# The inverse of the delta rule, on 128x128 matmuls or on blocks of 32 and 64 rows

## The chip, the cores and the metric

The kernel runs on one core of a Trainium2 chip. The metric is device time in microseconds of one execution. A core has TensorE (matmuls into PSUM; the profile shows its weight loads as PEld), VectorE (DVE), ScalarE (ACT), GpSimd (POOL) and SyncE (SP, which here only issues DMAs).

## The reference

A trunk of two layers on 256 tokens of width 2048, in float32. Layer 0 mixes the tokens by eight heads of a gated delta rule beside a pooling mixer, layer 1 by a convolution module; each is followed by a squared-ReLU MLP. The change touches the delta rule alone, of which this is the part that matters:

```python
def gated_delta_rule(q, k, v, g, beta):
    ...
    gamma = jnp.exp(jnp.where(causal, gc[..., :, None] - gc[..., None, :], -jnp.inf))
    kb = k * beta[..., None]
    a_mat = jnp.where(strict, jnp.einsum('bhnck,bhnmk->bhncm', kb, k) * gamma, 0.0)
    t_inv = lax.linalg.triangular_solve(a_mat + eye, jnp.broadcast_to(eye, a_mat.shape),
                                        left_side=True, lower=True, unit_diagonal=True)
    u = jnp.einsum('bhncm,bhnmv->bhncv', t_inv, v * beta[..., None])
    w = jnp.einsum('bhncm,bhnmk->bhnck', t_inv, kb * jnp.exp(gc)[..., None])
```

So each piece of tokens needs the inverse of a unit lower triangular matrix. The reference cuts the sequence into pieces of 64 tokens; the kernel uses pieces of 128, two per head.

## The kernel before

Weights stream from HBM as tiles `w` of 128x2048 (`load`, 1 MB each). ScalarE makes a rounded high part `wh`, VectorE the rest `wl`, in halves of 1024 columns. A `gemm` adds 48 passes of 256 columns into a PSUM bank `mm`: high by high, high by low, low by high, over 16 blocks of the contraction.

Layer 0's mixer is in `even`. The eight heads go in four rounds of two. A round has `keys` (projections and normalized keys), `front` (values, queries, gates), `inverse` and `finish` (the recurrence over the two pieces, and the head's output). The rounds overlap: the projections of the next round are computed while the inverse of this one runs. The order of all instructions on each engine is fixed when the program is built, by a scheduler with its own cost estimates; `inverse` and `finish` stand under `tc.high_priority()`. After the last round `pooling` follows; its eight gemms may run earlier, but what it writes as operand for the output projection lies in the same memory as the inverse's scratch tile `scr`, so that part comes after the last `finish`.

`inverse` handles four 128x128 matrices at once (two heads, two pieces), side by side in 512 columns. `a` is minus the strictly lower matrix, `aT` its transpose by TensorE. It keeps the inverse `t` and the transposed inverse `tT`, both full size. It starts with the diagonal blocks of 4 rows: `b` and `bT` are `a` and `aT` with all else masked out, and with their square `xs` the product (1+b)(1+b^2) is the inverse there. Then five levels double the block from 4 to 128 rows. On a level `xs` is `a` times `t` (bank `px`, copied by ScalarE), `pq` is `t` times `xs` and `pr` its transpose; two predicated copies on VectorE with masks from `msks` put the new blocks into `t` and `tT`. On the last level only `tT` is needed, as the weights of the two matmuls in `finish`. All of these matmuls are f32 with 128 rows and 128 columns of weights and 128 moving columns, which the program writes in groups of four (`ch<-scr 128x128`). The banks `ch` are two, used in turn.

Of the kernel before, what the change touches and what calls it, by code (L numbers as in the profile page):

```python
# [7 lines left out]
F32 = mybir.dt.float32  # L8
# [5 lines left out]
P = 128  # L14
SEQ = 256
# [3 lines left out]
EPS = 1e-6  # L19
BIG = 1e30  # L20
WINDOWS = (2, 4, 8, 16)
LEVELS = (4, 8, 16, 32, 64)

# [19 lines left out]


@with_exitstack
def trunk_kernel(ctx: ExitStack, tc: tile.TileContext, x_in, xT, vec, dwt, posts, ab, cst, msk, inv,
                 ew, eba, epw, ewo, ow, owo, mu, md, out):
    nc = tc.nc  # L50

    cp = ctx.enter_context(tc.tile_pool(name="cp", bufs=1))
# [20 lines left out]
        return op_a_tile[:, k, sl]  # L73

    vecs = cp.tile([P, V_COLS], F32, name="vecs")
    csts = cp.tile([P, 6, P], F32, name="csts")
    abs_ = cp.tile([P, 16], F32, name="abs_")
    invs = cp.tile([P, 4, 16], F32, name="invs")
    msks = cp.tile([P, 9, P], mybir.dt.uint8, name="msks")
    ident, triu, ones, pos, neg, blk = (csts[:, i, :] for i in range(6))  # L80
    mhalf = cp.tile([P, 1], F32, name="mhalf")
    nc.gpsimd.memset(mhalf, -0.5)

# [9 lines left out]
    def bank(tag):  # L93
        return pp.tile([P, 2 * SEQ], F32, tag=tag, name=tag, bufs=4 if tag == "mm" else 2)
# [4 lines left out]
    def stt(out_, a, s, b, op0=ALU.mult, op1=ALU.mult):  # L99
        return nc.vector.scalar_tensor_tensor(out_, a, s, b, op0=op0, op1=op1)  # L100

    def pin(ins):
        return tc.keep_in_program_order(ins)

    def mm(ps, lhsT, rhs, start=True, stop=True):
        nc.tensor.matmul(ps, lhsT, rhs, start=start, stop=stop)  # L106
# [206 lines left out]
    def first_operand(ep, src):  # L313
        w = wp.tile([P, D], F32, tag="w", name="w", bufs=2)
        wh = wp.tile([P, D], F32R, tag="wh", name="wh")
        wl = wp.tile([P, D], F32R, tag="wl", name="wl")
        xqs, cols = [], [slice(512 * i, 512 * i + 512) for i in range(4)]
        for i in range(4):
            xq = sc([P, 4, SEQ], "xq", pool=ep, bufs=4)
            nc.sync.dma_start(xq, xT[:, 4 * i:4 * i + 4, :])  # L320
            nc.sync.dma_start(w[:, cols[i]], src[:, cols[i]])
            xqs.append(xq)
        for k in range(KT):
            split(op_a, k, xqs[k // 4][:, k % 4, :], scale=v(V_MIX_PRE + k))
            if k % 4 == 3:
                c = cols[k // 4]
                nc.scalar.copy(wh[:, c], w[:, c])  # L327
                nc.vector.tensor_sub(wl[:, c], w[:, c], wh[:, c].bitcast(F32))
        return xqs, (wh, wl)
# [17 lines left out]
    def gate_weights():  # L347
        w = wp.tile([P, D], F32, tag="w", name="w", bufs=2)
        nc.sync.dma_start(w[:, :KT * 16], eba)
        wv = w[:, :KT * 16].rearrange("p (k m) -> p k m", m=16)  # L350
        wh = wp.tile([P, D], F32R, tag="wh", name="wh")
        wl = wp.tile([P, D], F32R, tag="wl", name="wl")
        nc.vector.memset(wh.bitcast(F32), 0.0)
        nc.gpsimd.memset(wl.bitcast(F32), 0.0)
        whv = wh.rearrange("p (k m) -> p k m", m=P)[:, :, :16]
        nc.scalar.copy(whv, wv)
        nc.vector.tensor_sub(wl.rearrange("p (k m) -> p k m", m=P)[:, :, :16], wv, whv.bitcast(F32))
        return wh, wl
# [94 lines left out]
    def heads(h0, r, ep, scr, obs, em, beta, nbeta, eg, ek, be):  # L453
# [6 lines left out]
        def quad(ap):  # L460
            return ap.rearrange("p (i t) -> p i t", i=4)

        def all4(mask):
            return mask.unsqueeze(1).to_broadcast([P, 4, P])

        kns, knTs = [], []
        a, aT, b, t = (scr[:, i] for i in range(4))
        spare = [scr[:, 6], scr[:, 7]]


        def keys(first=None):
# [35 lines left out]
        def inverse(tT):  # L507
            ps = bank("ch")
            for i in range(4):
                knT = knTs[i // 2][:, i % 2, :]  # L510
                mm(ps[:, i * P:(i + 1) * P], knT, knT)
            for i in range(4):
                h, c = h0 + i // 2, i % 2
                stt(a[:, i, :], ps[:, i * P:(i + 1) * P], nbeta[:, c, h:h + 1], em[:, h, 0, c, :])
            ps = bank("ch")
            for i in range(4):
                nc.tensor.transpose(ps[:, i * P:(i + 1) * P], a[:, i, :], ident)
            nc.scalar.copy(aT, quad(ps))

            bT, xs = spare  # L520
            nc.vector.tensor_mul(b, a, all4(blk))
            nc.vector.tensor_mul(bT, aT, all4(blk))
            nc.vector.tensor_add(t, b, all4(ident))
            nc.vector.tensor_add(tT, bT, all4(ident))
            ps = bank("ch")
            for i in range(4):
                mm(ps[:, i * P:(i + 1) * P], b[:, i, :], bT[:, i, :])
            nc.scalar.copy(xs, quad(ps))
            pq, pr = bank("ch"), bank("ch")
            for i in range(4):  # L530
                mm(pq[:, i * P:(i + 1) * P], xs[:, i, :], t[:, i, :])
            for i in range(4):
                mm(pr[:, i * P:(i + 1) * P], t[:, i, :], xs[:, i, :])
            nc.vector.tensor_add(t, t, quad(pq))
            nc.vector.tensor_add(tT, tT, quad(pr))

            for lv in range(len(LEVELS)):
                last = lv == len(LEVELS) - 1
                px = bank("ch")
                xs = spare[lv % 2]  # L540
                for i in range(4):
                    mm(px[:, i * P:(i + 1) * P], aT[:, i, :], t[:, i, :])
                nc.scalar.copy(xs, quad(px))  # L543
                if not last:
                    pq = bank("ch")
                    for i in range(4):
                        mm(pq[:, i * P:(i + 1) * P], tT[:, i, :], xs[:, i, :])
                    nc.vector.copy_predicated(t, all4(msks[:, lv, :]), quad(pq))
                pr = bank("ch")
                for i in range(4):  # L550
                    mm(pr[:, i * P:(i + 1) * P], xs[:, i, :], tT[:, i, :])
                nc.vector.copy_predicated(tT, all4(msks[:, 4 + lv, :]), quad(pr))


        def finish(tT, tag):
            for hh in range(2):
# [35 lines left out]
                split(obs, h, y)  # L592

        return keys, front, inverse, finish

    def pooling(r, ep, op_b):
# [30 lines left out]
    def even():  # L627
        with tc.tile_pool(name="fp", bufs=2) as fp:
            wh, wl = gate_weights()
            xqs, first = first_operand(fp, ew[HEADS])  # L630
            r = first_norm(fp, xqs)
        with tc.tile_pool(name="ep", bufs=2) as ep:
            scr = cp.tile([P, 8, 4, P], F32, tag="op_b1", name="scr")
            decays, *gs = gates(r, wh, wl, ep)
            for h in range(2):
                decays(h, "ch")
            mraw = scr[:, :3].rearrange("p i c t -> p (i c t)")[:, :9 * P].rearrange("p (i t) -> p i t", t=P)
            pin(nc.gpsimd.dma_start(mraw, msk))
            pin(nc.gpsimd.tensor_copy(msks, mraw))
            lower = cp.tile([P, KT // 2, 2 * SEQ], F32R, tag="op_b0", name="op_b0")  # L640
            rounds = [heads(h, r, ep, scr, lambda k, sl: lower[:, k, sl], *gs) for h in range(0, HEADS, 2)]
            rounds[0][0](first)
            for i, (_, front, inverse, finish) in enumerate(rounds):
                front()
                if i + 1 < len(rounds):
                    for h in range(max(2 * i + 2, 2), 2 * i + 4):
                        decays(h, "sm")
                    rounds[i + 1][0]()
                with tc.high_priority():
                    inverse(scr[:, 4 + i % 2])  # L650
                    finish(scr[:, 4 + i % 2], "ch" if i + 1 == len(rounds) else "sm")
            upper = cp.tile([P, KT // 2, 2 * SEQ], F32R, tag="op_b1", name="op_b1")

            def op_b(k, sl):
                return (lower if k < KT // 2 else upper)[:, k % (KT // 2), sl]

            pooling(r, ep, op_b)
        return op_b
# [125 lines left out]

    nc.gpsimd.dma_start(vecs[:, :V_NEAR], vec[:, :V_NEAR])
    nc.gpsimd.dma_start(csts, cst)
    nc.gpsimd.dma_start(abs_, ab)
    nc.gpsimd.dma_start(invs, inv)
    xd = dp.tile([P, 2, D], F32, name="xd", bufs=1)
# [97 lines left out]
```

## Time and profile before

| | |
|---|---|
| median of three runs | 2254.94 us (2253.87 to 2256.69) |
| the profiled execution | 2253.11 us, its span 2251.3 us |
| granted TensorE clock, mean | 0.987 |
| TensorE busy | 2194.6 us, 97% |
| VectorE, ScalarE busy | 1350.2 us (60%), 1030.2 us (46%) |
| DMA | 414.46 MB, mean 184 GB/s |

All times inside a profile count from the start of the span. A row of a group gives line, engine, operation, tiles written and read, shapes and count. A TensorE row of the form `128*32 128x256` has 128 rows and 32 columns of weights, and a result of 256 columns. One f32 matmul leaves two records, one fp32r matmul one. In a table by stretch the columns are the stretch, its length, then busy time and count for TensorE, weight loads, VectorE, ScalarE and GpSimd, the granted clock, the DMA share and GB/s. A bracket at a timeline row's end is the time that the engine sat idle before it and who released it.

### The profile page before, as it was taken

Reading aid. Unit: us, or ns where it says so; the run is one execution under the profiler, and the core shown is the slowest. Engines: PE = TensorE matmul, PEld = TensorE weight load, DVE = VectorE, ACT = ScalarE, POOL = GpSimd, SP = SyncE. Lnnn points to the kernel's source line nnn. Section 1 sums busy time; section 2 is a strip of 40 time slices with the busy share of each in tenths; the row PEclk is TensorE's granted clock in tenths of the full one; section 3 lists DMA queues with packets and bytes.
Section 4 is the critical chain, followed back from the end, with each engine's and each line's share of the span. In section 5 each row is a group of like instructions: output and inputs, shape, how many; then the busy total and the mean of one; then the engine's idle time right before and its main releaser. Section 6 shows DMA issues by size and latency. Waiting matters only on the chain.

```text
span 2251.3 us, 32079 instructions
## 1 busy us (share of the span) xinstructions
PE 2194.6 (97%) x13228; PEld 1915.9 (85%) x13228; DVE 1350.2 (60%) x1926; ACT 1030.2 (46%) x1569; POOL 125.5 (6%) x200
## 2 busy tenths in 40 slices
PE   8999998999999999999999999799999999999997
PEld 8999997888888888888878999588888888888886
DVE  7767674576456456556556777557645645655654
ACT  6646554454444344334434333445444434443442
POOL 3201000000000000000002222000000000000000
PEclk9999999999999999999999999899999999999999
DMA  6433334645555555555547887454555555555553
GB/s 220 144 130 132 116 129 155 238 169 205 188 188 189 197 193 187 188 190 194 195 150 229 228 228 220 163 208 172 202 196 194 188 187 189 192 197 188 188 189 110
DMA packets 67378, 414.46 MB, mean 184 GB/s; under 512 B 13952, under 2 KB 14112, under 8 KB 20000
## 3 DMA queue, kind: packets, MB, share of 16 engines
q1 hardware_dynamic: 55440, 391.27, 48.9%
q0 software_dynamic: 11792, 21.15, 4.1%
q8 instruction: 103, 1.69, 0.3%
q14 instruction: 43, 0.35, 0.0%
HBM read 405.75 MB, written 6.55 MB: 183 GB/s over the span
## 4 chain that ended last, share of the span: by engine, by line
PE 94%; DVE 2%; issue 1%; ACT 1%; DMA 1%; POOL 0%; POOLq 0%; DVEq 0%; SPq 0%; ACTq 0%
PE mm L106 87%; PE ch L106 3%; PE sm L705 2%; PE sm L106 1%; DVE wl L131 1%; DMA w<-ew 0%; DVE op_a L100 0%; ACT L97 0%; PE sm L441 0%; PE sm L233 0%; PE ch L233 0%; ACT wh L125 0%; DMA xq<-xT 0%; POOL r L190 0%; DVE x L100 0%
## 5 line engine op out<-in xcount | busy, mean ns | idle before, releaser
L131 DVE TENSOR_TENSOR wl<-w,wh 128x1024 fp32r<-128x1024 f32 x720 | 853.7, 1223 | 580.6 <-ACT wh L125 579.7
L106 PE MATMUL mm<-op_a,wh 128*128 128x256 f32 (+1 forms) x4352 | 1148.7, 337 | 0.3 <-ACT wh L327 0.3
L125 ACT CAST wh<-w 128x1024 fp32r<-128x1024 f32 x720 | 720.3, 1049 | 675.7 <-PE mm L106 558.1
L106 PE MATMUL mm<-op_a,wl 128*128 128x256 f32 x3200 | 901.5, 282 | 0.0
L106 PEld LDWEIGHTS mm<-op_a,wh 128*128 128x128 f32 x4352 | 745.1, 189 | 92.8 <-issue 5.5
L106 PE MATMUL mm<-wh,op_b 128*128 128x512 f32 x2560 | 796.0, 392 | 4.9 <-ACT op_b L97 4.5
L106 PEld LDWEIGHTS mm<-op_a,wl 128*128 128x128 f32 x3200 | 604.7, 189 | 3.6 <-issue 2.4
L106 PEld LDWEIGHTS mm<-wh,op_b 128*128 128x128 f32 x2560 | 481.3, 188 | 108.4 <-ACT op_b L97 5.1
L106 PE MATMUL mm<-wl,op_b 128*128 128x512 f32 x1280 | 498.9, 390 | 0.0
L106 PEld LDWEIGHTS mm<-wl,op_b 128*128 128x128 f32 x1280 | 240.9, 188 | 51.4 <-DVE wl L131 0.2
L97 ACT ACTIVATE op_b<-f 128x256 fp32r<-128x256 f32 x128 | 53.3, 418 | 229.6 <-DVE f L100 229.6
L190 POOL TENSOR_TENSOR r<-m,mhalf 128x1 f32<-128x1 f32 x8 | 6.1, 766 | 1615.2 <-DVE m L257 1615.2
L186 DVE TENSOR_TENSOR op_b<-f,op_b 128x256 fp32r<-128x256 f32 x128 | 54.2, 425 | 55.3 <-ACT op_b L97 55.3
L106 PE MATMUL ch<-scr 128*128 128x128 f32 x544 | 68.7, 275 | 0.3 <-ACT scr L543 0.3
L106 PEld LDWEIGHTS ch<-scr 128*128 128x128 f32 x544 | 64.8, 191 | 0.6 <-ACT scr L543 0.5
L705 PE MATMUL sm<-us,wd 128*32 128x256 f32 x752 | 50.5, 394 | 8.8 <-issue 8.8
L300 DVE TENSOR_TENSOR big<-mm,big 128x512 f32<-128x512 f32 x48 | 33.0, 687 | 42.9 <-PE mm L106 42.9
L100 DVE SCALAR_TENSOR_TENSOR f<-h 128x256 f32<-128x256 f32 x128 | 54.2, 425 | 4.0
L289 DVE TENSOR_TENSOR h<-mm,hl 128x256 f32<-128x256 f32 x128 | 53.3, 418 | 0.0
L100 DVE SCALAR_TENSOR_TENSOR near<-u,vecs,near 128x256 f32<-128x256 f32 x104 | 49.2, 480 | 0.9
L705 PEld LDWEIGHTS sm<-us,wd 128*32 128x32 f32 x752 | 25.1, 112 | 26.6 <-issue 12.1
L162 ACT COPY hl<-mm 128x256 f32<-128x256 f32 x128 | 46.1, 362 | 2.7 <-DVE h L289 2.2
(242 smaller groups left out, 893.9 us busy)
## 6 DMA issues: line engine op xcount, KB each, us to landing
w<-mu SPq DMA_DIRECT2D x128, 1024.0 KB, 4.8
w<-md SPq DMA_DIRECT2D x128, 1024.0 KB, 4.8
w<-ew SPq DMA_DIRECT2D x39, 1024.0 KB, 4.8
w<-ow SPq DMA_DIRECT2D x32, 1024.0 KB, 5.4
w<-ewo SPq DMA_DIRECT2D x16, 1024.0 KB, 4.9
w<-owo SPq DMA_DIRECT2D x16, 1024.0 KB, 4.9
us<-ud POOLq DMA_DIRECT2D x64, 140.5 KB, 7.8
wd<-dwt POOLq DMA_DIRECT2D x14, 384.0 KB, 5.9
```

The lines of the kernel that those rows point to most:

```text
L97: return nc.scalar.activation(out_, in_, func, bias=bias, scale=scale, **kw)
L100: return nc.vector.scalar_tensor_tensor(out_, a, s, b, op0=op0, op1=op1)
L106: nc.tensor.matmul(ps, lhsT, rhs, start=start, stop=stop)
L125: ins = nc.scalar.copy(wh[:, c], w[:, c])
L131: ins = nc.vector.tensor_sub(wl[:, c], w[:, c], wh[:, c].bitcast(F32))
L162: nc.scalar.copy(s, ps[:, SEQ:])
L186: return first, nc.vector.tensor_sub(op(k, LO), src, hi)
L190: nc.gpsimd.tensor_tensor(dst, m, mhalf.to_broadcast(m.shape), op=ALU.pow)
L289: nc.vector.tensor_add(h, hh, s)
L300: nc.vector.tensor_add(m, ps[c], m)
L705: nc.tensor.matmul(ps[32 * g:32 * g + 32, :SEQ], wd[:, i, g, :], us[:, g, lo:lo + SEQ], start=i == skip, stop=i == GROUPS - 1, tile_positi ...
```

## The change

The inverse no longer works on whole 128x128 matrices. The four diagonal blocks of 32 rows of each matrix are kept in a compact form: `t32`, 128 partitions by four matrices by 32 columns. They start from blocks of two rows, whose inverse needs no matmul (a constant `sub` picks the one element below the diagonal, `diag` adds the ones). Levels 2, 4, 8 and 16 then work within the blocks, on tiles of 32 rows by 32 columns of the tensor array: `tile_mm` gives the place of the tile, and the four blocks of one matrix lie on the four tiles of the array's diagonal. The transposed factor `tT32` is no longer computed by matmuls of its own, but by a transpose of 32x32 blocks on VectorE after each predicated copy. So a level has 32 matmuls in two groups of 16 instead of 12 of full size, and its copies cover 128 columns instead of 512.

Two steps then join blocks. The 32-row blocks are joined to 64 (one group of 8 and one of 12 tile matmuls), and the 64-row blocks to 128 by two groups of four matmuls on tiles of 64 by 64; in each step only the block off the diagonal is computed, and copied to its place in `tl` or `tT`. The other parts of `tT` and `tl` are never written, so one memset on GpSimd clears them once. The masks shrink from nine of 128 columns to four of 32; the constants lose one matrix and gain the small input `blk`, loaded by a DMA of its own on GpSimd's queue.

```diff
-LEVELS = (4, 8, 16, 32, 64)
+LEVELS = (2, 4, 8, 16)
+ROWS32 = [slice(b, b + 32) for b in range(0, 128, 32)]
...
+        def tile_mm(rows, cols, ps, lhsT, rhs):
+            nc.tensor.matmul(ps[cols], lhsT[rows], rhs[rows], start=True, stop=True,
+                             tile_position=(rows.start, cols.start))
...
-            bT, xs = spare
-            nc.vector.tensor_mul(b, a, all4(blk))
-            nc.vector.tensor_mul(bT, aT, all4(blk))
-            nc.vector.tensor_add(t, b, all4(ident))
-            nc.vector.tensor_add(tT, bT, all4(ident))
-            ps = bank("ch")
+            for b in ROWS32:
+                nc.vector.tensor_mul(t32[b], a[b, :, b], sub[b].unsqueeze(1).to_broadcast([32, 4, 32]))
+            nc.vector.tensor_add(t32, t32, diag.unsqueeze(1).to_broadcast([P, 4, 32]))
+            nc.vector.transpose(flat(tT32), flat(t32))
+            for lv in range(len(LEVELS)):
+                px = bank("ch")
+                for i in range(4):
+                    for b in ROWS32:
+                        tile_mm(b, b, px[:, 32 * i:32 * i + 32], aT[:, i, b], t32[:, i, :])
+                nc.scalar.copy(flat(x32), px[:, :P])
+                pq = bank("ch")
+                for i in range(4):
+                    for b in ROWS32:
+                        tile_mm(b, b, pq[:, 32 * i:32 * i + 32], tT32[:, i, :], x32[:, i, :])
+                nc.vector.copy_predicated(t32, msks[:, lv, :].unsqueeze(1).to_broadcast([P, 4, 32]), quad(pq[:, :P]))
+                nc.vector.transpose(flat(tT32), flat(t32))
+
+            for b in ROWS32:
+                nc.scalar.copy(tT[b, :, b], tT32[b])
+            px, pr = bank("ch"), bank("ch")
+            pairs = ((ROWS32[0], ROWS32[1]), (ROWS32[2], ROWS32[3]))
+            for b in ROWS32[:2]:
+                nc.vector.tensor_copy(tl[b, :, b], t32[b])
             for i in range(4):
-                mm(ps[:, i * P:(i + 1) * P], b[:, i, :], bT[:, i, :])
-            nc.scalar.copy(xs, quad(ps))
-            pq, pr = bank("ch"), bank("ch")
+                for lo, hi in pairs:
+                    tile_mm(lo, hi, px[:, 32 * i:32 * i + 32], aT[:, i, hi], t32[:, i, :])
+            for _, hi in pairs:
+                nc.scalar.copy(x64[hi, :, :32], quad(px[hi, :P]))
             for i in range(4):
-                mm(pq[:, i * P:(i + 1) * P], xs[:, i, :], t[:, i, :])
-            for i in range(4):
-                mm(pr[:, i * P:(i + 1) * P], t[:, i, :], xs[:, i, :])
-            nc.vector.tensor_add(t, t, quad(pq))
-            nc.vector.tensor_add(tT, tT, quad(pr))
-
-            for lv in range(len(LEVELS)):
-                last = lv == len(LEVELS) - 1
-                px = bank("ch")
-                xs = spare[lv % 2]
-                for i in range(4):
-                    mm(px[:, i * P:(i + 1) * P], aT[:, i, :], t[:, i, :])
-                nc.scalar.copy(xs, quad(px))
-                if not last:
-                    pq = bank("ch")
-                    for i in range(4):
-                        mm(pq[:, i * P:(i + 1) * P], tT[:, i, :], xs[:, i, :])
-                    nc.vector.copy_predicated(t, all4(msks[:, lv, :]), quad(pq))
-                pr = bank("ch")
-                for i in range(4):
-                    mm(pr[:, i * P:(i + 1) * P], xs[:, i, :], tT[:, i, :])
-                nc.vector.copy_predicated(tT, all4(msks[:, 4 + lv, :]), quad(pr))
+                for lo, hi in pairs:
+                    tile_mm(hi, lo, pr[:, 32 * i:32 * i + 32], x64[:, i, :32], tT32[:, i, :])
+                tile_mm(pairs[0][1], pairs[0][1], pr[:, 32 * i:32 * i + 32], tT32[:, i, :], x64[:, i, :32])
+            nc.vector.tensor_copy(tl[ROWS32[1], :, ROWS32[0]], quad(pr[ROWS32[1], :P]))
+            for lo, hi in pairs:
+                nc.scalar.copy(tT[lo, :, hi], quad(pr[lo, :P]))
+
+            lo, hi = slice(0, 64), slice(64, P)
+            px = bank("ch")
+            for i in range(4):
+                tile_mm(lo, hi, px[:, 64 * i:64 * i + 64], aT[:, i, hi], tl[:, i, :64])
+            nc.scalar.copy(x64[hi, :, 32:96], quad(px[hi, :SEQ]))
+            pr = bank("ch")
+            for i in range(4):
+                tile_mm(hi, lo, pr[:, 64 * i:64 * i + 64], x64[:, i, 32:96], tT[:, i, hi])
+            nc.vector.tensor_copy(tT[lo, :, hi], quad(pr[lo, :SEQ]))
...
-            mraw = scr[:, :3].rearrange("p i c t -> p (i c t)")[:, :9 * P].rearrange("p (i t) -> p i t", t=P)
+            mraw = scr[:, 0, 0, :].rearrange("p (i t) -> p i t", t=32)
             pin(nc.gpsimd.dma_start(mraw, msk))
             pin(nc.gpsimd.tensor_copy(msks, mraw))
+            nc.gpsimd.memset(scr[:, 3:6], 0.0)
```

The scheduler also orders the work around it anew. On VectorE, in the first round, a level stood so before (the weight subtraction `wl` belongs to the next gemm, `t_...` to the short convolution of a projection):

```order
L100 SCALAR_TENSOR_TENSOR t_1096<-t_1094,vecs,t_1096 128x253
L548 COPY_PREDICATED scr<-msks,ch 128x512
L552 COPY_PREDICATED scr<-msks,ch 128x512
L428 TENSOR_TENSOR t_1393<-mm,rrow 128x256
L204 TENSOR_SCALAR mc<-ss 128x2
L131 TENSOR_TENSOR wl<-w,wh 128x1024 x2
```

and now:

```order
L134 TENSOR_TENSOR wl<-w,wh 128x1024
L546 COPY_PREDICATED scr<-msks,ch 128x128
L134 TENSOR_TENSOR wl<-w,wh 128x1024
L103 SCALAR_TENSOR_TENSOR t_1099<-t_1097,vecs,t_1099 128x255
L547 STREAM_TRANSPOSE scr<-scr 128x128
L207 TENSOR_SCALAR mc<-ss 128x2
```

The two predicated copies that followed each other have become a copy and a transpose, with a weight subtraction between them.

On TensorE, at the end of the last round, where `finish` begins (`ch<-vb,scr` is its first matmul) and the gemms of `pooling` are the only other work, the order was:

```order
L106 MATMUL mm<-op_a,wl 128x256
L106 MATMUL ch<-scr 128x128 x4
L106 MATMUL mm<-op_a,wh 128x256 x2
L106 MATMUL mm<-op_a,wl 128x256
L106 MATMUL ch<-scr 128x128 x4
L106 MATMUL ch<-vb,scr 128x128
L106 MATMUL ch<-scr,kb 128x128
```

and now:

```order
L109 MATMUL mm<-op_a,wh 128x256
L478 MATMUL ch<-scr 64x64 x4
L109 MATMUL mm<-op_a,wh 128x256
L109 MATMUL mm<-op_a,wl 128x256
L109 MATMUL mm<-op_a,wh 128x256 x2
L109 MATMUL mm<-op_a,wl 128x256
L109 MATMUL mm<-op_a,wh 128x256 x2
L109 MATMUL mm<-op_a,wl 128x256
L109 MATMUL ch<-vb,scr 128x128
L109 MATMUL ch<-scr,kb 128x128
```

Before, nothing stood between the inverse's last group and `finish`; now eight gemm passes do.

More of the change, by code (lines that the diff above doesn't have):

```diff
@@ L47, in trunk_kernel @@
 @with_exitstack
-def trunk_kernel(ctx: ExitStack, tc: tile.TileContext, x_in, xT, vec, dwt, posts, ab, cst, msk, inv,
+def trunk_kernel(ctx: ExitStack, tc: tile.TileContext, x_in, xT, vec, dwt, posts, ab, cst, blk, msk, inv,
                  ew, eba, epw, ewo, ow, owo, mu, md, out):
@@ L75, in trunk_kernel @@
     vecs = cp.tile([P, V_COLS], F32, name="vecs")
-    csts = cp.tile([P, 6, P], F32, name="csts")
+    csts = cp.tile([P, 5, P], F32, name="csts")
+    blks = cp.tile([P, 2, 32], F32, name="blks")
     abs_ = cp.tile([P, 16], F32, name="abs_")
     invs = cp.tile([P, 4, 16], F32, name="invs")
-    msks = cp.tile([P, 9, P], mybir.dt.uint8, name="msks")
-    ident, triu, ones, pos, neg, blk = (csts[:, i, :] for i in range(6))
+    msks = cp.tile([P, len(LEVELS), 32], mybir.dt.uint8, name="msks")
+    ident, triu, ones, pos, neg = (csts[:, i, :] for i in range(5))
+    diag, sub = (blks[:, i, :] for i in range(2))
     mhalf = cp.tile([P, 1], F32, name="mhalf")
@@ L466, in heads, with flat @@
         kns, knTs = [], []
-        a, aT, b, t = (scr[:, i] for i in range(4))
-        spare = [scr[:, 6], scr[:, 7]]
+        a, aT, tl, x64 = (scr[:, i] for i in (0, 1, 3, 6))
+        t32, tT32, x32 = (scr[:, 2, i, :].rearrange("p (i t) -> p i t", i=4) for i in range(3))
+        def flat(ap):
+            return ap.rearrange("p i t -> p (i t)")
+        def tile_mm(rows, cols, ps, lhsT, rhs):
+            nc.tensor.matmul(ps[cols], lhsT[rows], rhs[rows], start=True, stop=True,
+                             tile_position=(rows.start, cols.start))
         def keys(first=None):
@@ L786, in trunk_kernel @@
     nc.gpsimd.dma_start(csts, cst)
+    nc.gpsimd.dma_start(blks, blk)
     nc.gpsimd.dma_start(abs_, ab)
@@ L850 @@
     i, j = np.arange(P)[:, None], np.arange(P)[None, :]
-    cst = np.stack([i == j, i <= j, np.ones((P, P)), -BIG * (i <= j), -BIG * (j < i), i // 4 == j // 4],
+    cst = np.stack([i == j, i <= j, np.ones((P, P)), -BIG * (i <= j), -BIG * (j < i)],
                    axis=1).astype(np.float32)
-    low = [(i // (2 * s) == j // (2 * s)) & (i % (2 * s) >= s) & (j % (2 * s) < s) for s in LEVELS]
-    msk = np.stack(low[:4] + [m.T for m in low], axis=1).astype(np.float32)
+    i, j = i % 32, np.arange(32)[None, :]
+    blk = np.stack([i == j, (i == j + 1) & (i % 2 == 1)], axis=1).astype(np.float32)
+    msk = np.stack([(i // (2 * s) == j // (2 * s)) & (i % (2 * s) >= s) & (j % (2 * s) < s) for s in LEVELS],
+                   axis=1).astype(np.float32)
     inv = np.stack([1.0 / np.minimum(np.arange(1, 17), w) for w in WINDOWS]).astype(np.float32)
@@ L869 @@
         "xT": x.T.reshape(KT, P, SEQ).transpose(1, 0, 2),
-        "vec": vec, "dwt": dwt, "posts": posts, "ab": ab, "cst": cst, "msk": msk, "inv": inv,
+        "vec": vec, "dwt": dwt, "posts": posts, "ab": ab, "cst": cst, "blk": blk, "msk": msk, "inv": inv,
         "ew": tiled(w_in), "eba": eba, "epw": epw, "ewo": blocks(a["even_w_out"][0]),
```

## The prediction

> **What bounds the kernel now.** I read the page's busy line first, then the busy time by stretch to find the stage that the change touches, then the same stretch restricted to the inverse's scratch tile `scr`.
>
> ```profile
> PE 2194.6 (97%) x13228; PEld 1915.9 (85%) x13228; DVE 1350.2 (60%) x1926; ACT 1030.2 (46%) x1569; POOL 125.5 (6%) x200
> 75.00:345.00 270.00, 269.69 (x2314) 269.06 (x2312) 185.50 (x345) 149.37 (x330) 23.40 (x38) 1.00 0.36 129
> 75.00:345.00 270.00, 77.19 (x588) 71.05 (x588) 45.84 (x75) 16.16 (x28) 0.00 (x0) 1.00 0.36 129
> ```
>
> The four inverses run between 75 and 345 us. There TensorE (second column of figures) is busy 269.69 of 270 us at full clock (1.00); VectorE has 185.5, ScalarE 149.4, the DMA share is 0.36. So this stage is as long as TensorE's work in it, and every microsecond of matmul taken out shortens it, as long as nobody else becomes late. The third line says that 588 of its matmul passes touch `scr`. (An f32 matmul leaves two pass records: 272 in the program, 544 in the next rows.)
>
> ```profile
> L106 PE MATMUL ch<-scr x544: 270/275/377, 82.6 to 345.9; 128*128 128x128 f32 x182
> L543 ACT COPY scr<-ch x20: 564/584/588, 93.0 to 344.4; 128x512 f32<-128x512 f32 x20
> L552 DVE COPY_PREDICATED scr<-msks,ch x20: 717/740/746, 97.9 to 347.2; 128x512 f32<-128x512 uint8 x20
> L100 DVE SCALAR_TENSOR_TENSOR scr<-ch,nbeta,big x16: 340/342/350, 75.5 to 289.0; 128x128 f32<-128x128 f32 x16
> 96.09 1.78 PE ch L106 x16
> 98.43 1.65 PE mm L106 x14
> 100.08 0.89 PE ch L106 x8
> ```
>
> The last three lines are pieces of the chain that ended last: it runs through TensorE, inverse groups (`ch`) alternating with gemm passes (`mm`). A group of 16 passes occupies 1.78 us, so a 128x128 pass costs 0.111 us of the path; the 275 ns of a single record overlap with its neighbours. A gemm pass costs 1.65/14 = 0.118 us. No wait stands between them, because each group starts well after its operand:
>
> ```profile
> 93.05 0.59 ACT L543 COPY scr<-ch 128x512 f32<-128x512 f32 x1 [0.21 <-PE ch L106]
> 95.92 1.95 PE L106 MATMUL ch<-scr 128*128 128x128 f32 x16
> 97.91 0.74 DVE L552 COPY_PREDICATED scr<-msks,ch 128x512 f32<-128x512 uint8 x1 [0.16 <-PE ch L106]
> 99.92 0.49 PE L106 MATMUL ch<-scr 128*128 128x128 f32 x3
> ```
>
> Copy ended 93.64, its matmuls began 95.92: 2.3 us to spare. Predicated copy ended 98.65, next group 99.92: 1.3 us.
>
> **What is removed.** Per round (two heads) 12 matmuls of the 4-row start, 12 on each of four levels and 8 on the last: 68 matmuls, 136 passes x 0.111 = 15.1 us of TensorE; four rounds 60.4 us, all on the path.
>
> **What is added on TensorE.** Per round 8 groups (four levels, `px` and `pq`) of 16 matmuls on 32x32 tiles, one group of 8, one of 12, and two of 4 on 64x64 tiles: 156 matmuls, 312 passes, 12 groups. No row shows a 32x32 matmul. The nearest is the convolution of the other layer, L705, on 128x32 tiles:
>
> ```profile
> 1308.84 0.27 PE L106 MATMUL mm<-op_a,wl 128*128 128x256 f32 x1
> 1309.04 2.80 PE L705 MATMUL sm<-us,wd 128*32 128x256 f32 x48
> 1311.77 0.50 PE L106 MATMUL mm<-op_a,wh 128*128 128x256 f32 x2
> 1309.04:1311.67 2.63, 2.63 (x48) 1.45 (x48) 1.00 0.89 359
> L705 PEld LDWEIGHTS sm<-us,wd x752: 106/109/178, 1213.3 to 1425.7; 128*32 128x32 f32 x188
> 1323.32 0.16 PEld L705 LDWEIGHTS sm<-us,wd 128*32 128x32 f32 x8
> 1323.32 0.42 PE L705 MATMUL sm<-us,wd 128*32 128x256 f32 x4
> ```
>
> Three prices come from it. First, streaming: 48 passes in 2.63 us are 12 sets of four column strips at 0.219 us, that is, four tiles do run side by side. With 32 moving columns instead of 256 a set takes an eighth, 0.027 us. Second, the switch of the array between whole and tiled: in, 1309.04 - 1308.84 = 0.20 us where 0.118 is normal; out, 1311.77 - 1311.67 = 0.10 us. Together 0.18 us a group. Third, the feed: a small pass needs a weight load and a matmul record, 64 records for a group of 16 matmuls. The last two rows show eight loads covering 0.16 us where one takes 0.106, so twelve records began within 0.05 us: 4.5 ns each when they lie ready in the queue. The steady row gives 96 records in 2.63 us, 27 ns each, where streaming set the pace; so 27 is an upper bound there. A group of 16 is then between 64 x 4.5 = 0.29 us and 64 x 27 = 1.75 us. I take 0.55 us, 8.6 ns a record: nearer the lower end, because the rows above give the queue 1.3 to 2.3 us to fill after the operand is there. Per round: 8 x 0.55 = 4.4; the group of 8 (32 records) 0.28; that of 12 (48 records) 0.41; the 64x64 groups run one tile at a time with 64 columns, 8 passes x 0.055 = 0.44 each, 0.88; switches 12 x 0.18 = 2.16. Sum 8.1 us. Saved 15.1 - 8.1 = 7.0 us a round, 28 us in all. With the ends: 0.29 makes the round 5.8 us (with 0.22 and 0.29 for the groups of 8 and 12) and saves 37 us in all; 1.75 makes it 19.2 us and loses 16 us.
>
> A rule of the Trainium skill to weigh: "TensorE: Matmul & The Clock Gate", section "Part 3: Packing small matmuls — row/col tiling", has a pack of tiles take one matmul plus about 4 ns for each further tile, close to the 4.5 ns of the queued row. By it a group would stand at the lower end and the time would be about 2216 us, an estimate from that page.
>
> **The tail.** In the last round nothing is left to hide behind:
>
> ```profile
> 344.73 0.42 DVE L605 TENSOR_TENSOR t<-mm,rrow 128x256 f32<-128x256 f32 x1 [1.62 <-PE mm L106]
> 345.02 1.16 PE L106 MATMUL ch<-scr 128*128 128x128 f32 x8 [0.32 <-ACT scr L543]
> 346.09 1.22 DVE L131 TENSOR_TENSOR wl<-w,wh 128x1024 fp32r<-128x1024 f32 x1
> 347.23 0.72 DVE L552 COPY_PREDICATED scr<-msks,ch 128x512 f32<-128x512 uint8 x1
> 348.00 0.49 PE L106 MATMUL ch<-vb,scr 128*128 128x128 f32 x2 [1.82 <-DVE scr L552]
> ```
>
> TensorE waits 0.32 and 1.82 us, the latter since the predicated copy stood behind a 1.22 us low-part subtraction. In the new order 8 gemm passes (0.94 us) stand between the last group and `finish`, and a 64x256 copy with no subtraction right ahead of it replaces the predicated one. By the first row of this fence such a read of 256 columns takes 0.42 us, so I count the wait as covered: -2.1 us. Late next is `finish` itself, which is unchanged.
>
> **The other engines, counted at nothing.** VectorE loses nine predicated copies of 0.74 us and four masked products a round; it gains four 128x128 predicated copies, five transposes, some 32-row products and copies, each near the 0.34 us of the 128x128 row. It falls by about 6 us a round, with 84 us of slack in the stage. The transpose has no row: at least the 0.16 us of the smallest operation (first row below), at most the 0.74 us of the 512-column copy if it ran at a quarter of the rate. Its cover is the px matmuls and ScalarE's copy that the next `pq` needs as well, and the 1.3 us; beyond 1.3 us TensorE would wait four times a round. ScalarE's copies shrink from 0.58 us, but there are more of them: about even. Queued behind each of these are the weight casts of the next gemm, which gain from the shorter ones.
>
> On GpSimd the change adds one DMA issue and a memset of 1536 columns near the start, and shrinks the mask's cast (the other rows):
>
> ```profile
> 99.39 0.16 DVE L204 TENSOR_SCALAR mc<-ss 128x2 f32<-128x2 f32 x1
> 2.58 0.56 POOL L787 DMA_DIRECT2D abs__72<-ab  x1
> 3.64 1.85 POOL L354 MEMSET wl<- 128x2048 f32 x1
> 12.04 5.68 POOL L340 TENSOR_TENSOR acc<-acc,sq 128x256 f32<-128x256 f32 x6 [3.17 <-ACT sq L97]
> 67.27 1.13 POOL L639 CAST msks<-scr 128x1152 uint8<-128x1152 f32 x1
> ```
>
> 0.56 + 1.85 x 1536/2048 = 1.9 us later for the sums `acc`, which the 3.17 us wait before the second batch swallows; without it the row statistics would come 1.9 us later. The cast ends before the first inverse as it did. SP's queue is untouched.
>
> Sum: -28 - 2.1 = -30 us. The profiled execution has a span of 2251.3 and a time of 2253.11 us, 1.8 us under the median 2254.94; I carry the difference to the median: **2225 us**.
>
> **Rivals.** 1) *Small passes cost more, but less than the old ones* (feed of 15 to 21 ns a record, or tiles that take turns). 592 records in groups of 32x32 x 21 = 12.4, plus 0.88 and 2.16, is 15.5 us a round, no gain but the tail's. At 15 ns: 11.9 us, -15 us in all, 2240. Tiles in turn, 32 x 0.027 = 0.86 us a group, give 11.2 us and 2237, the edge between this and the forecast. For it: 27 ns is all that the steady row proves. Against it: four strips ran side by side. Range 2240 to 2252.
> 2) *The sequencer cannot feed them: slower.* From 21 ns a record, 42 ns a pass, TensorE has more to do than before. If a small pass cost what a 128x128 pass costs, 0.111 us, a round would be 312 x 0.111 + 2.2 = 36.8 us, +85 us, 2340. For it: nothing shows records below 27 ns for long, and each group is fresh work after a wait. Against it: the 12 records in 0.05 us, and the time to queue. The Trainium skill, same page, section "Wait — 56ns, not 53.3ns?", names about 62 ns per matmul where the sequencer decodes in microcode. As a mechanism here: 312 x 0.062 + 2.2 = 21.5 us a round, +24 us, about 2279, an estimate from that page. The L705 row stands against it in part: 48 passes in 2.63 us are 55 ns each, but some may have been queued ahead.
> 3) *A late operand.* TensorE's order is fixed; if the two-step chain on VectorE (predicated copy, then transpose, with a 1.22 us subtraction between) outlasts its gemm cover, TensorE idles. 0.5 us in each of 48 groups is 24 us and leaves 2249. Against it: 1.3 us of slack and shorter operations.
>
> **How the numbers follow.** Forecast (0.29 to about 1 us a group) 0.68, 2213 to 2240. Rival 1: 0.13. Rival 2: 0.09. Rival 3: 0.08, half of it no change. 0.02 below. A difference under 0.2%, 4.5 us, cannot be told from none by this measurement. Faster: 0.68 + 0.13 + 0.02, less a little of rival 1's upper edge, plus a third of rival 3: 0.85; same 0.06; slower 0.09. The range 2212 to 2253 leaves out rival 2 and the outer parts of the others.
>
> **What would show it.** Right: the stretch that holds the inverses is about 28 us shorter with TensorE still near 100%; 32x32 groups lie 0.5 to 0.6 us apart from first to last pass, each with a step of about 0.2 us around it; `finish` in the last round starts without the 1.82 us wait. Wrong: groups above 1.3 us; new TensorE waits on the transposes or on `x32`; or the stage keeps its length because VectorE's weight subtractions come late.

## The result and the profile after

The changed kernel takes **2214.94 us** in the median (four runs, 2212.28 to 2216.25), the kernel before 2255.08 us beside it (2253.87 to 2256.69). The ratio is 0.9816, 95% interval 0.9804 to 0.9829: 1.8% faster, some 40 us. The forecast was 2225 us with a range of 2212 to 2253. The profiled execution of the changed kernel took 2215.81 us, with a span of 2214.0.

First its busy line from the page, then its busy time by stretch (length, then busy us and count of PE, PEld, DVE, ACT, POOL, then clock, DMA share, GB/s), the last line restricted to the instructions that touch `scr`:

```profile
PE 2161.1 (98%) x13932; PEld 1874.7 (85%) x13932; DVE 1328.3 (60%) x1938; ACT 1027.2 (46%) x1593; POOL 129.3 (6%) x202
```

```profile
75.00:310.00 235.00, 235.00 (x2993) 225.85 (x2992) 159.39 (x343) 144.90 (x349) 22.22 (x37) 1.00 0.41 142
75.00:310.00 235.00, 32.30 (x1296) 24.68 (x1296) 22.07 (x78) 16.26 (x55) 0.00 (x0) 1.00 0.41 142
```

The stage of the inverses now ends near 310 us where it ended near 345, and TensorE is as full in it as before (235.00 of 235 us). What touches `scr` keeps it busy for 32.30 us instead of 77.19, with 1296 passes instead of 588. VectorE's share on `scr` fell from 45.84 to 22.07 us.

The groups of instructions on `scr` that answer to those shown of before (count, then min/median/max in ns):

```profile
L478 PE MATMUL ch<-scr x1248: 191/191/267, 76.3 to 309.4; 32*32 32x32 f32 x169, 64*64 64x64 f32 x10
L541 ACT COPY scr<-ch x16: 244/264/267, 76.8 to 290.2; 128x128 f32<-128x128 f32 x16
L546 DVE COPY_PREDICATED scr<-msks,ch x16: 293/298/306, 80.7 to 293.4; 128x128 f32<-128x128 uint8 x16
L547 DVE STREAM_TRANSPOSE scr<-scr x16: 303/306/311, 83.0 to 294.1; 128x128 f32<-128x128 f32 x16
```

The transpose that no row of before could price takes 0.306 us.

Pieces of the chain that ended last, and one group with its neighbours from the timeline (start, length; a record lasts about 0.19 us past its start, so starts are what counts):

```profile
83.44 0.38 PE ch L478 x32
83.83 2.80 PE mm L109 x22
86.62 0.38 PE ch L478 x32
```

```profile
90.53 0.28 PE L109 MATMUL mm<-op_a,wl 128*128 128x256 f32 x1
90.74 0.45 PE L478 MATMUL ch<-scr 32*32 32x32 f32 x32
91.12 0.50 PE L109 MATMUL mm<-op_a,wh 128*128 128x256 f32 x2
```

The chain still runs through TensorE alone. A group of sixteen 32x32 matmuls lies between 90.53 and 91.12: 0.59 us from one gemm pass to the next, 0.118 of which that pass would have taken anyway, so **0.475 us** net. Its 32 starts spread over 0.45 - 0.19 = 0.26 us; the step in is 0.21 us (0.09 above normal), the step out 0.12. The 0.475 leaves one thing out: the two gemm passes behind the group take 0.50 us in the last row, where two such passes elsewhere take 0.40. In the list of starts the first of them, at 91.125, holds TensorE for 0.225 us instead of 0.118.

**Where the time came from.** The cleanest place to compare is the first matmul of the projection that follows the stage, the first start in these rows of before and after:

```profile
L106 PE MATMUL mm<-wh,op_b x2560: 387/389/796, 359.3 to 2238.6; 128*128 128x512 f32 x197
...
L109 PE MATMUL mm<-wh,op_b x2560: 387/389/794, 323.5 to 2202.4; 128*128 128x512 f32 x197
```

It comes 35.9 us earlier (359.31 and 323.45 in the list of starts), and the last start of the program 36.2 us earlier: nearly all of the 37.3 us by which the spans differ is made by then. I sorted the distances from each matmul's start to the next, up to that place, by what they are next to (summed from the trace):

| distances between starts, us | before | after | difference |
|---|---|---|---|
| next to a matmul of an inverse | 66.8 | 30.7 | -36.1 |
| of that, waits of the tail (0.32 + 1.82) | 2.1 | 0 | -2.1 |
| other gaps over 0.35 us, 40 to 76 us | 4.4 | 0 | -4.4 |
| other gaps over 0.35 us, the last `finish` | 6.1 | 8.0 | +1.9 |
| everything else | 282.0 | 284.8 | +2.8 |
| of that, the pass behind each of the 49 groups | 7.9 | 10.3 | +2.4 |

So the inverses' TensorE time fell by 34.0 us (36.1 less the tail's waits of 2.1), waits ahead of the first inverse by 4.4, and the tail gave back what it had gained. Of the 34.0 us, 2.4 come back in the last row: the pass right behind a group takes 0.21 us on average to the next start, in the kernel before 0.16. The rest of "everything else" is 1.1 us more of start and gaps before 40 us, and 0.7 us less in all other passes.

**The tail.** TensorE's and ScalarE's timeline at the end of the last inverse:

```profile
308.95 0.68 PE L478 MATMUL ch<-scr 64*64 64x64 f32 x8
309.56 0.39 PE L109 MATMUL mm<-op_a,wh 128*128 128x256 f32 x1
...
310.62 0.38 PE L109 MATMUL ch<-vb,scr 128*128 128x128 f32 x2
310.84 0.39 PE L109 MATMUL ch<-scr,kb 128*128 128x128 f32 x2
313.08 0.49 PE L109 MATMUL ch<-vn,kd 128*128 128x128 f32 x2 [1.85 <-ACT vn L591]
```

```profile
310.74 1.99 ACT L128 CAST wh<-w 128x1024 fp32r<-128x1024 f32 x2 [1.86 <-PE mm L109]
312.76 0.27 ACT L591 COPY vn<-ch 128x128 f32<-128x128 f32 x1
```

The gemm passes cover the copy as forecast: `finish` starts at 310.62 with no wait. But its next step needs the copy `vn`, and that stands on ScalarE behind two weight casts, which themselves had waited for the buffer that those gemm passes were reading. The 1.82 us came back as 1.85 us, one step later (before, the wait at that step was 0.35 us).

### The profile page after: what moved, and what is told of

It is laid out like the page before. It is cut to its first block, busy times and chain, and to the rows that moved or that the text cites. A ratio compares the mean times of both kernels' runs of the same rounds, so it can differ in the third digit from the quotient of the medians.

```text
span 2214.0 us, 33537 instructions
## 1 busy us (share of the span) xinstructions
PE 2161.1 (98%) x13932; PEld 1874.7 (85%) x13932; DVE 1328.3 (60%) x1938; ACT 1027.2 (46%) x1593; POOL 129.3 (6%) x202
## 3 DMA queue, kind: packets, MB, share of 16 engines
q1 hardware_dynamic: 55440, 391.27, 50.5%
## 4 chain that ended last, share of the span: by engine, by line
PE 95%; DVE 2%; ACT 1%; issue 1%; DMA 1%; POOL 0%; SPq 0%; POOLq 0%; DVEq 0%; ACTq 0%
PE mm L109 89%; PE sm L730 2%; PE sm L109 1%; PE ch L478 1%; PE ch L109 1%; DVE wl L134 1%; PE sm L444 0%; DMA w<-ew 0%; DMA xq<-xT 0%; ACT wh L128 0%; PE sm L236 0%; ACT op_a L100 0%; PE ch L236 0%; POOL r L193 0%; DVE x L103 0%
## 5 line engine op out<-in xcount | busy, mean ns | idle before, releaser
L708 POOL DMA_DIRECT2D us<-ud x64 | 43.8, 691 | 38.4 <-DMA ud<-u 35.0
L730 PEld LDWEIGHTS sm<-us,wd 128*32 128x32 f32 x752 | 23.7, 111 | 25.7 <-issue 10.3
L103 DVE SCALAR_TENSOR_TENSOR t<-t,vecs,t 128x255 f32<-128x255 f32 (+2 forms) x72 | 34.1, 474 | 2.1 <-ACT t L100 1.3
```

Of the source, the lines that this page charges most:

```text
L708: nc.gpsimd.dma_start(us[:, g, :FAR], bass.AP(tensor=ud.tensor, offset=ud.offset + 32 * g * ROW, ap=[[1, 4], [ROW, 32], [1, FAR]]))
L730: nc.tensor.matmul(ps[32 * g:32 * g + 32, :SEQ], wd[:, i, g, :], us[:, g, lo:lo + SEQ], start=i == skip, stop=i == GROUPS - 1, tile_positi ...
```

## The experiments

For each, "up to the projection" is the first start of the projection's matmuls, and "next to inverses" the first row of the table above; in the changed kernel they are 323.45 and 30.7 us. Against the kernel before, its ratio is 0.9816.

### What sets the length of a group: `e1_turns`

```
-for i in range(4):
-    for b in ROWS32:
+for b in ROWS32:
+    for i in range(4):
         tile_mm(b, b, px[...], aT[:, i, b], t32[:, i, :])   # pq likewise
```

> The same 32x32 matmuls, issued block by block (the four matrices of one block one behind the other) instead of matrix by matrix. Theory (a group lasts as long as the passes of ONE tile, 8 at 35.5 ns = 0.28 us, because the four tiles run side by side, and the queue is kept in order): now the tiles take turns, 32 x 35.5 ns = 1.14 us first to last pass instead of 0.26, +0.87 us in each of 32 groups, +28 us in all: 2243 us. Rival (records are what costs, 8 ns a pass, whichever tile they go to): no change, 2215 us, groups of 0.26 us. Rival (each tile draws from a queue of its own): no change either.

```profile
90.49 0.28 PE L109 MATMUL mm<-op_a,wh 128*128 128x256 f32 x1
90.70 0.89 PE L478 MATMUL ch<-scr 32*32 32x32 f32 x32
91.52 0.44 PE L444 MATMUL sm<-csts,kvq 128*128 128x128 f32 x2
```

2236.71 us median, ratio 0.9915 (0.9900 to 0.9931). The same 32 passes now spread over 0.89 - 0.19 = 0.70 us instead of 0.26: the order of issue alone costs 0.44 us a group, 14 us in 32 groups. So records by themselves do not cost 8 ns each, and tiles do not draw from queues of their own; both rivals fall. But the turns are not strict, which would have been 1.14 us. The records do not name their tile, but in every group as many of them as it has tiles last 212 ns instead of 191, and in the changed kernel these are the first four: a tile's first pass. In the list of starts (82.667, 82.720, 82.752, 82.783, 82.815, then 82.821 with 212 ns) a tile's passes lie 32 ns apart from the second on, and the next tile's first pass starts 0.154 us after the former tile's first, while three of that one's eight are still to come. Three times 0.154 and the last tile's own 0.24 make the 0.70. The rest of the loss up to the projection (21.6 us in all) is mostly gaps of 2.5 us before the first inverse, of 1.6 us within the stage, and new waits of 1.3 and 2.4 us in the tail. That the longer groups caused them is not shown.

### Passes or steps: `e2_twice`

```
-for i in range(4):
+for i in [*range(4), *range(4)]:      # px and pq, the four 32-row levels
```

> Each of the 32 groups of 32x32 matmuls is issued twice over within the group (32 matmuls, 64 passes, the same products again). Theory (35.5 ns for a pass of a tile, and a step in and out that is paid once a group): 16 passes a tile, +0.28 us a group, +9.1 us: 2224 us, groups of 0.55 us first to last pass. Rival (the prediction's feed of 8.6 ns a record, 0.55 us a group, which the first trace hid by a queue that was already full): the second half has no time to queue, +0.55 us a group or more, +17.6 us: 2232 us or above. Rival (the passes are hidden in the step of the array): no change, 2215 us.

```profile
95.73 0.28 PE L109 MATMUL mm<-op_a,wl 128*128 128x256 f32 x1
95.94 0.75 PE L478 MATMUL ch<-scr 32*32 32x32 f32 x64
96.62 0.50 PE L109 MATMUL mm<-op_a,wh 128*128 128x256 f32 x2
```

2227.67 us, ratio 0.9879 (0.9864 to 0.9894). Twice the passes take 0.56 us instead of 0.26, with the same step in (0.21) and out: +0.30 us a group, and next to inverses 40.3 against 30.7 us, +9.6, where the theory had 9.1. The second half of the group had less time to lie ready, and runs at nearly the same pace as the first. It shows another pattern, though: from about the 40th start on, passes come in pairs every 16.6 ns instead of in fours every 32 ns. So whether the tiles or the feed of records set the pace there is open; the feed is at least as fast as this. The prediction's fear that the feed holds only while the queue is full is answered: eight further passes on each of four tiles cost 0.30 us, 9.4 ns a pass, 4.7 ns a record. Up to the projection it is +8.5 us; the median is higher by 11.4 once both are taken against the kernel before beside them (2256.40 here).

### Tiles or columns: `e3_whole`

```
-for i in range(4):
-    for b in ROWS32:
-        tile_mm(b, b, px[...], aT[:, i, b], t32[:, i, :])
+for i in range(4):
+    mm(px[:, 32 * i:32 * i + 32], aT[:, i, :], t32[:, i, :])   # pq with flat(tT32)
```

> The 32x32 levels on the whole array: 4 matmuls of 128x128 weights and 32 columns in place of the 16 on 32x32 tiles (the blocks outside the diagonal are not masked, so the values differ). Theory (a whole-array pass costs about 0.111 us whether 128 or 32 columns move, since 128 columns took 0.111 and 256 took 0.118): 8 x 0.111 = 0.89 us a group against 0.475 net of the tiled one, +13 us: 2228 us. Rival (the columns set the pace; the gain comes from 32 columns, not from the tiles): 8 passes of 0.03 to 0.055 us and no step of the array, 0.24 to 0.44 us a group, -1 to -7.5 us: 2207 to 2214 us.

```profile
92.71 0.28 PE L109 MATMUL mm<-op_a,wl 128*128 128x256 f32 x1
92.83 0.97 PE L109 MATMUL ch<-scr 128*128 128x32 f32 x8
93.64 0.48 PE L109 MATMUL mm<-op_a,wh 128*128 128x256 f32 x2
```

2231.90 us, ratio 0.9898 (0.9884 to 0.9912). (This kernel does not mask the blocks off the diagonal, so its values are not those of the inverse.) There is no step into tiles now (92.71 to 92.83 is the normal 0.12), and still the group costs 0.93 - 0.12 = 0.81 us against 0.475. In the list of starts the passes lie 0.111 us apart from the second on, as with 128 columns. So a fourth of the columns is worth nothing on whole-array weights; the gain is that a pass on a 32x32 tile is shorter, and that four run at once. Next to inverses it is 44.3 us: 10.7 us in the groups, and 3.0 us of new waits in the tail.

### The other half of the change: `e5_factors`

```
+pr = bank("ch")                       # 16 more: x32^T times tT32
+for i in range(4):
+    for b in ROWS32:
+        tile_mm(b, b, pr[...], x32[:, i, :], tT32[:, i, :])
 nc.vector.copy_predicated(t32, msks[:, lv, ...], quad(pq[:, :P]))
+nc.vector.copy_predicated(tT32, msks[:, 4 + lv, ...], quad(pr[:, :P]))
-nc.vector.transpose(flat(tT32), flat(t32))
```

> The changed kernel with the transposed 32-row factors computed by a third group of 16 matmuls on each of the four levels, with a predicated copy under a transposed mask, in place of the 32x32 transposes on VectorE: this undoes that part of the change alone. Theory (what counts is TensorE's time, 0.475 us net a group; VectorE has time to spare for either): 16 more groups, +7.6 us up to the projection that follows the stage, about 2222 us. Rival (the transposes are late operands that TensorE already pays for in the changed kernel): the third group is paid back, no change or a gain, 2215 us or less. Rival (the transposes carry the change's gain): far more than 7.6 us.

```profile
93.89 0.75 PE L478 MATMUL ch<-scr 32*32 32x32 f32 x64
...
96.71 0.45 PE L478 MATMUL ch<-scr 32*32 32x32 f32 x32
```

2225.22 us, ratio 0.9861 (0.9844 to 0.9878), beside 2218.58 for the changed kernel on the same chip. Next to inverses +4.8 us. Up to the projection it is +4.8 too, but by coincidence: 2.5 us of new gaps before and in the stage stand against gaps in the tail that are 3.2 us shorter. I had expected 7.6, and missed that `pr` stands right behind `pq` (64 passes in one row), so the array's step is paid once for both: 16 x 0.30 = 4.8. By TensorE's time the transposes on VectorE are therefore worth about 5 of the change's 34 us; most is the tiling.

### Fewer groups: `e6_doubling`

```
+nc.vector.tensor_copy(pw[b], a[b, :, b])                 # for each b; pt holds pw and t32 side by side
+nc.vector.tensor_add(t32, pw, diag)
+for lv in range(5):
+    lo, n = (1, 1) if lv == 4 else (0, 1 if lv == 0 else 2)
...
+            tile_mm(b, b, po[:, :, i, :], aT[:, i, b] if lv == 0 else tT32[:, i, :], pt[:, lo:lo + n, i, :])
+    if lv < 4:
+        nc.scalar.copy(flat(pw), ps[:, :P])
+        nc.vector.transpose(flat(tT32), flat(pw))
+    if lv > 0:
+        nc.vector.tensor_add(flat(t32), flat(t32), ps[:, (n - 1) * P:n * P])
+nc.vector.transpose(flat(tT32), flat(t32))
```

> The same 32-row inverses by five groups a round in place of eight: powers of the block by doubling, each group multiplying the transposed power by the power and by the product so far side by side (64 columns in groups 2 to 4, 32 in the first and last). The mask and its transfer go. Theory (a group costs a step of about 0.2 us in and out, and 8 passes a tile at a price set by the columns, 32 ns for 32 and about 55 ns for 64, from the 219 ns that 256 took): 2 x 0.475 + 3 x 0.66 = 2.9 us a round against 3.8, -3.5 us: about 2211.5 us. Rival (the weights set the price of a pass on a tile, as on the whole array where 32 columns took the same 0.111 us as 128): 64 columns cost no more, 5 x 0.475 = 2.4 us, -5.7 us: 2209 us. Rival (the copy and the transpose that follow each group come late, now that fewer groups lie between them): TensorE waits in the stage, no gain.

```profile
77.33 0.45 PE L479 MATMUL ch<-scr 32*32 32x32 f32 x32
77.72 0.70 PE L108 MATMUL sm<-gu,csts 128*128 128x256 f32 x2
...
80.86 0.65 PE L479 MATMUL ch<-scr 32*32 32x64 f32 x32
81.44 0.70 PE L108 MATMUL sm<-gu,csts 128*128 128x256 f32 x2
```

With 64 columns the starts spread over 0.435 us instead of 0.263, a tile's passes 55 ns apart from the second on: the columns' price, as the theory had it, and not that of the weights. Net of one normal pass for each group, TensorE's time for the inverses falls by 3.5 us, from 24.9 to 21.4, as forecast. Up to the projection's first pass 0.7 us of it is left, at its last pass 2.1; 1.1 us are lost before the first inverse, and the rest of the difference I did not trace further. The time is 2220.99 us, ratio 0.9841 (0.9818 to 0.9863), beside 2218.58 and 0.9830: no gain that can be measured.

### The tail: `e7_tail`

```
+if tag == "ch" and hh == 0:
+    nc.vector.tensor_copy(vn[:, 0, :], ps[:, :P])
+    nc.vector.tensor_scalar(nw, ps[:, P:2 * P], -1.0, 0.0, op0=ALU.mult, op1=ALU.add)
+else: ...                             # ScalarE as before
```

> The changed kernel with the first two copies of the last round's finish (vn and nw of its first head) moved from ScalarE, where they stood behind two weight casts, to VectorE. Theory (the wait of 1.85 us after the inverse is a matter of that queue alone): it shrinks to about 0.5 us, and the copy st behind it, still on ScalarE, is the next to come late, about 0.5 us earlier than before; the projection's first matmul comes 0.5 us earlier. Rival (TensorE waits at the projection for the weights anyway): its later passes start at the same time as before, nothing is gained by then.

```profile
313.59 0.49 PE L109 MATMUL ch<-vn,kd 128*128 128x128 f32 x2 [0.38 <-DVE vn L592]
...
315.37 0.49 PE L109 MATMUL ch<-st,nw 128*128 128x128 f32 x2 [1.07 <-ACT st L599]
315.69 0.39 PE L109 MATMUL ch<-vn,at 128*128 128x128 f32 x2
```

The last of these rows in the changed kernel:

```profile
314.51 0.63 PE L109 MATMUL ch<-vn,at 128*128 128x128 f32 x2
```

(The first three rows are TensorE's timeline of this run; everything stands 2 us later in this execution, see below.) The wait of 1.85 us falls to 0.38, and the next copy on ScalarE, `st`, is late by 1.07. Two waits of 1.45 us in place of one of 1.85: the queue was the cause, and the chain behind it is serial. Relative to the 2.0 us by which this execution was late before the inverses, the projection's first pass comes 1.0 us earlier and its last 1.2, so it is not swallowed by the wait for weights. Not all of the 1.0 us is waiting. The six passes from `st,nw` up to the second `vn,at` take 315.37 to 316.21, 0.84 us, here, and 313.92 to 315.36, 1.44 us, in the changed kernel. The granted clock there is 1.00 from 315.50 to 317.00 here, and 0.50 from 314.00 to 315.50 in the changed kernel, where an f32 pass takes 0.213 us instead of 0.111. So some 0.6 us are the clock, which fell later in this run, and some 0.5 the shorter waits. The single execution took 2216.76 us; 1 us is too small to be seen in it.

### The waits before the first inverse: `e4_oldmask` and `after2`

```
-msks = cp.tile([P, len(LEVELS), 32], mybir.dt.uint8, name="msks")
+msks = cp.tile([P, 36, 32], mybir.dt.uint8, name="msks")     # transfer and cast of 1152 columns
```

> The changed kernel with the mask transfer and its cast at their old size (576 KB, 1152 columns), of which only the first 128 columns are used. It asks where the 3.5 us come from that the changed kernel gains before its first inverse. Theory A (the smaller transfer and cast): TensorE waits of about 3.3 us come back between 40 and 75 us, 2218 us. Theory B (another order of instructions in that stage, in which TensorE always has a gemm pass to run): no wait comes back, 2215 us, within 1 us.

What TensorE waited for between 30 and 75 us (us in total, times, longest), in the kernel before, in this one, and in `e7_tail`:

```profile
PE sm L106 <- ACT vb L97: 1.5, 1, 1.5
PE sm L441 <- ACT kvq L97: 0.9, 1, 0.9
PE ch L106 <- POOL gu L415: 0.5, 1, 0.5
PE ch L106 <- ACT knT L479: 0.4, 1, 0.4
```

```profile
PE sm L444 <- ACT kvq L100: 1.5, 1, 1.5
PE ch L370 <- issue: 0.5, 1, 0.5
```

```profile
PE sm L444 <- ACT kvq L100: 1.3, 1, 1.3
PE ch L370 <- issue: 0.4, 1, 0.4
```

From GpSimd's timeline of `e4_oldmask`, the issue of the mask's transfer; and the transfer of weights that stands in the chain ahead of the wait on `kvq`, in `e4_oldmask` and in `e7_tail`:

```profile
64.36 0.62 POOL L662 DMA_DIRECT2D scr<-msk  x1
```

```profile
39.94 6.34 DMA w<-ew
```

```profile
40.08 6.07 DMA w<-ew
```

At first sight theory A: 2220.42 us, ratio 0.9841 (0.9828 to 0.9854), and the wait on `kvq` is back. But in the timeline it ends at 50.5 us, and the mask's transfer is issued at 64.4. And `e7_tail`, whose mask is small and whose edit lies in the last `finish`, shows the same wait, with the same transfer of weights ahead of it (6.07 and 6.34 us). So that wait is not the mask's: theory A falls. In the five variants that have this wait it grows with that transfer: 5.20 us and a wait of 0.38 (`e3_whole`), 6.05 and 1.12 (`e5_factors`), 6.07 and 1.25 (`e7_tail`), 6.34 and 1.51 (`e4_oldmask`), 6.42 and 1.58 (`e1_turns`). What makes the transfer longer is open. The other three waits of before, on `vb`, `gu` and `knT`, appear neither in the changed kernel nor in these two, and no run undid the order of instructions there. That the order is their cause is argued, not shown.

> The changed kernel again, unaltered, as the common base of the runs beside it: 2215 us within 2 us of its first median, or the same ratio to the kernel before, 0.98.

2218.58 us, ratio 0.9830 (0.9815 to 0.9846). The rows show what may differ between two executions of the same kernel; first its projection, then the stretch from 1180 to 1430 us (the convolution of the other layer) in the first and in this execution:

```profile
L109 PE MATMUL mm<-wh,op_b x2560: 387/389/796, 323.5 to 2208.1; 128*128 128x512 f32 x197
```

```profile
1180.00:1430.00 250.00, 234.23 (x2159) 201.66 (x2158) 170.49 (x292) 87.26 (x119) 56.00 (x95) 0.96 0.72 212
```

```profile
1180.00:1430.00 250.00, 232.69 (x2135) 199.83 (x2136) 167.12 (x288) 86.23 (x116) 55.87 (x95) 0.95 0.72 210
```

Up to the projection the two agree within 0.1 us; of the 5.7 us by which this one ends later, 3.8 arise in the convolution, at a granted clock of 0.95 instead of 0.96 and with TensorE 1.5 us less busy, and 1.3 before it. The same spread stands between the 40 us of the first medians, the 37.5 of these, and the 36 up to the projection. So differences of 5 us between medians here are read with caution. Up to the projection this one pair agrees to a tenth, and differences there are read to a few tenths, apart from the transfer at 40 us.

## Why the prediction was right, and where its sizes were off

The mechanism holds: the stage is as long as TensorE's work in it, the change makes that work shorter, and nothing else became late inside the stage. By its steps:

- **What is removed.** Forecast 60.4 us. By the distances between starts it was 58.9 (the 64.7 of the table without waits, less a normal pass for each of 49 groups).
- **What is added: the term that was mis-sized.** Forecast 8.1 us a round, 32.4 in all; measured 24.9, or 27.3 with the 2.4 us of the passes behind the groups. The 64x64 groups (0.44 us forecast, 0.46 measured) and the group of 8 matmuls (0.28 and 0.25) were right. The group of 12 was priced at 0.41 us and takes 0.256, the groups of 16 at 0.55 us and take 0.263, since I let the feed of records set the pace, at 8.6 ns. What paces a group is the longest run of passes on one tile: eight, 53 ns from the first to the second, then 32 ns each. Two tiles (the group of 8) take 0.249 us, three 0.256 and four 0.263, with twice the records of two. The lower end of my bounds, 0.29 us from 4.5 ns a record, comes near, but by luck, for with half the records a group is as long.
- **The step of the array** was right in the two parts that I counted: 0.09 us in, and 0.09 us out beyond the last pass's own 32 ns, against 0.20 less 0.118, and 0.10. A third part I put at nothing without a reason, the pass behind the group, which takes 0.22 us instead of 0.118. It is not the tiles alone that cost this: in `e3_whole` it is 0.20 us behind whole-array groups of 32 columns. The prediction's own row shows it: the two gemm passes at 1311.77 took 0.50 us.
- **The rule of the Trainium skill** that I weighed there ("TensorE: Matmul & The Clock Gate", section "Part 3: Packing small matmuls — row/col tiling": one matmul's span plus about 4 ns for a further tile) gave 2216 us and came nearest. The rows agree in kind, with (0.263 - 0.249)/2 = 7 ns for a further tile.
- **The tail.** Forecast -2.1 us, "I count the wait as covered". The wait was covered, but I looked for what is late next only in TensorE's order, not in ScalarE's queue, where the casts stood ahead of `vn`: the waits of 0.32 and 1.82 us went, the one on `vn` grew from 0.35 to 1.85, and by the distances between starts (-2.14 and +1.87) -0.3 us is left in place of -2.1.
- **Unforeseen: -4.4 us ahead of the first inverse**, where I had counted nothing but GpSimd's 1.9 us as swallowed. Those do not show: the 193rd gemm pass starts at 37.01 us against 36.89. That gain is luck, and not a firm one: gaps of 0.7 to 2.5 us come back there in five of the variants above, among them three whose edits lie elsewhere (`e1_turns`, `e3_whole`, `e7_tail`).
- **The other engines at nothing.** Right: the transpose costs 0.306 us and no wait on it shows in the stage.
- **The sum.** -34.0 in the inverses, -0.3 in the tail, -4.4 ahead, and +2.8 in the spacing of the other matmuls make -35.9 us, against the -30 forecast; the medians differ by 40. The lower end of the groups' price made 2216 us, so no term of the prediction stands behind the lowest part of its range, where the measured 2214.94 lies; without the 4.4 us above the time would be about 2219.
- **The rivals.** Dearer small passes, a sequencer that cannot feed them and late operands all fail on the same rows: 0.475 us a group, TensorE busy for 235.00 of 235 us, and no wait of TensorE between 75 and 310 us. The price that the Trainium skill gives for the second one where the sequencer decodes in microcode, some 62 ns a matmul (same page, section "Wait — 56ns, not 53.3ns?"), is not met here: the 16 further matmuls of a group in `e2_twice` took 0.30 us, 19 ns each.

## What to carry to other kernels

Where a stage is full of TensorE work and the matmuls are small, count passes on the busiest tile and steps of the array, not matmuls: issue round-robin over the tiles, put groups that use the same tiling behind one another, and take the shape of the tile, not only the number of columns, as the price of a pass. When a wait is said to be covered, follow the next instruction's operand into the queue of the engine that makes it.

## What the runs showed of the hardware

- An f32 pass on a 32x32 tile repeats after 32 ns with 32 columns and 55 ns with 64; on a 64x64 tile with 64 columns after 58 ns; with whole-array weights after 111 ns, with 32 columns as with 128. On the tiles the second pass comes later, 53, 80 and 107 ns after the first.
- Up to four such tiles overlap, their starts some 7 ns apart, if the program alternates between them. When it finishes one tile first, the next starts 0.154 us later, before the last three of the former's eight passes (`e1_turns`).
- The step from whole-array to tiled matmuls costs 0.09 us in, and 0.09 us out beyond the last pass's own time (0.121, 0.144 and 0.148 us to the next start, where passes repeat after 32, 55 and 58 ns), with 8 to 64 passes between. The gemm pass behind it then takes 0.22 us instead of 0.118 (0.20 behind the whole-array groups of `e3_whole`).
- In the tail, after waits of TensorE, the granted clock is 0.50 for some 10 to 14 us, and an f32 pass then takes 0.213 us instead of 0.111.
